# Starting places of the split weights: one fixed place against eight in turn, 32 bytes apart

## The chip, the cores and the metric

The kernel runs on one core of one Trainium2 chip. The metric is the device time of one execution in microseconds (us), taken over several runs. Engines are named as in the profile: PE is the matrix engine (PEld its weight loads), DVE the vector engine, ACT the scalar engine, POOL the general-purpose engine, SP the engine whose queue issues most transfers.

## The reference

One layer of a hybrid decoder: a half-step SwiGLU block, a token mixer of two attentions merged by gates, and a second half-step SwiGLU block, in float32. 256 tokens and 16 meta tokens in front; width 2048, inner width 5632, eight heads of 128 for each attention.

```python
def _swiglu(x, w_gate, w_up, w_down):
    return (jax.nn.silu(x @ w_gate) * (x @ w_up)) @ w_down

def _hybrid_mixer(xn, w_in, b_forget, fox_q_norm, fox_k_norm, w_branch_fox, w_branch_sb, w_out):
    proj = xn @ w_in
    fq, fk, fv, f_logit, sq, sk, sv, g_fox, g_sb = jnp.split(proj, IN_SPLIT_POINTS, axis=-1)
    ...
    merged = jax.nn.sigmoid(g_fox) * (o_fox @ w_branch_fox) + jax.nn.sigmoid(g_sb) * (o_sb @ w_branch_sb)
    return merged @ w_out

    h = h + 0.5 * _swiglu(_rmsnorm(h, ffn1_norm), ffn1_w_gate, ffn1_w_up, ffn1_w_down)
    h = h + _hybrid_mixer(_rmsnorm(h, mix_norm), w_in, b_forget, ...)
    h = h + 0.5 * _swiglu(_rmsnorm(h, ffn2_norm), ffn2_w_gate, ffn2_w_up, ffn2_w_down)
```

## The kernel before

Each float32 product is made of three matmuls. Every operand is split into a high part (rounded to the matrix engine's fp32r type) and a low part (the rest), and `wh x xh`, `wl x xh` and `wh x xl` are summed in PSUM. ACT writes the high part and DVE the low one (`split`, L164 and L165).

All the weights are cut into *units* of 128 rows by 1024 values (two row tiles of 512 columns, as a rule), 753 in all, listed in the order of use (`units`). Three steps run over that list: `load` brings a unit into a `raw` tile (five buffers, SP's queue), `split_unit` makes its parts `wh` and `wl` (three buffers each), and `products` issues its matmuls at L944; `ahead` keeps six loads and two splits ahead of the products. Between matmuls `tick` lets the evacuations, the attention heads and the transposes of other stages go on in small steps. The tile framework orders each engine's instructions and sets the semaphores.

There are three kinds of blocks, and so of matmuls at L944:

- features on PSUM's partitions, 272 tokens: the weight is stationary, 272 columns of an activation part move (FFN1, keys and values);
- the same with 256 tokens (`wide`): `wh` is multiplied with both activation parts in one matmul of 512 columns, `wl` with the high part in one of 256 (queries, `w_out`);
- tokens on the partitions (`by_token`): the activation is stationary, 512 columns of the weight move (gates, branches, FFN2).

Activations lie in slots of one pool, `vals` (25 buffers of 4352 bytes in each partition, tag `v`). A slot holds two tiles, each with a high and a low part behind one another, of 272 columns (the norms of FFN1 and of the mixer) or of 256 (the branches' inputs, FFN2). The gate and query blocks read the mixer's norm, so 272-column parts, though they use 256 tokens. In SBUF the pool of constants comes first, then `vals`, then the weights' pool (`raw`, `wh`, `wl`, 4096 bytes a buffer), then temporaries.

The constants hold an identity and a matrix of ones twice, in float32 (`ident`, `ones`) and in fp32r (`identr`, `onesr`, copied by DVE at L136 and L137), and the first norm's gains apart from the others (`grow1`, `gcol1`). The start is ordered by hand: warm-up matmuls (L293), the transpose of the gains (L297), transposes of x (L312) and of the meta tokens (L303), and the first block's products (L914).

Of the kernel before, what the change touches and what calls it, by code (L numbers as in the profile page):

```python
# [16 lines left out]
P = 128  # L17
# [5 lines left out]
NM = 16  # L23
# [24 lines left out]
def hybrid_layer(ctx: ExitStack, tc: tile.TileContext, x, meta_tokens, ffn1_norm, ffn1_w_gate, ffn1_w_up,  # L48
# [47 lines left out]
            tick()  # L96


    ident = const([P, P], F32, "ident")
    make_identity(nc, ident)  # L100
    ones = const([P, P], F32, "ones")
    nc.gpsimd.memset(ones[:], 1.0)
    eps_c = const([P, 1], F32, "eps")
    nc.gpsimd.memset(eps_c[:], EPS)
    grow = const([64, P], F32, "grow")
    grow1 = const([16, P], F32, "grow1")
    nc.scalar.dma_start(grow1[:], ffn1_norm.rearrange("o (k p) -> (o k) p", p=P))
    for i, g in enumerate((ffn1_norm, mix_norm, ffn2_norm)):
        nc.gpsimd.dma_start(grow[16 * i:16 * i + 16, :], g.rearrange("o (k p) -> (o k) p", p=P))
    nc.gpsimd.dma_start(grow[48:56, :], fox_q_norm[0])  # L110
    nc.gpsimd.dma_start(grow[56:64, :], fox_k_norm[0])
# [4 lines left out]
    def tables():  # L116
        return tc.keep_in_program_order(act.preload_act_table_set(LN_EXP)).ins

    gcol1 = const([P, 16], F32, "gcol1")
    gcol = const([P, 64], F32, "gcol")  # L120
    gq = const([P, 8], F32, "gq")

    identr = const([P, P], F32R, "identr")
    onesr = const([P, P], F32R, "onesr")
    smask = const([P, 2, NR], F32R, "smask")
    urev = const([P, P], F32R, "urev")
    urevm = const([P, P], F32R, "urevm")
# [2 lines left out]
    def other_constants():  # L130
        yield 8
        g_ps = aux()
        pe.transpose(g_ps[:, :64], grow[:], ident[:64, :64])
        dve.tensor_copy(gcol[:], g_ps[:, :64])
        dve.tensor_scalar(gq[:], gcol[:, 48:56], SCALE, None, op0=ALU.mult)
        tc.keep_in_program_order(dve.tensor_copy(identr[:], ident[:]))  # L136
        tc.keep_in_program_order(dve.tensor_copy(onesr[:], ones[:]))  # L137
        tc.keep_in_program_order(dve.tensor_scalar(negone[:], ones[:], -1.0, None, op0=ALU.mult))
        yield 4
        t = temp([P, 2, NT], F32, "F3")  # L140
        nc.gpsimd.memset(t[:], 0.0)
        for i in range(2):
            nc.gpsimd.affine_select(t[:, i, :NR], t[:, i, :NR], pattern=[[1, NR]], compare_op=ALU.is_gt,
                                    fill=NEG, base=-128 * i, channel_multiplier=-1)
        tc.keep_in_program_order(dve.tensor_copy(smask[:], t[:, :, :NR]))
        t = temp([P, 2, NT], F32, "F3")
        nc.gpsimd.memset(t[:, :, :P], 0.0)
        nc.gpsimd.memset(t[:, 0, :P], -1.0)
        nc.gpsimd.affine_select(t[:, 0, :P], t[:, 0, :P], pattern=[[-1, P]], compare_op=ALU.is_ge,
                                fill=0.0, base=0, channel_multiplier=1)  # L150
        for p0 in (0, 32):
            m = t[p0:p0 + 32, 1, :P]
            nc.gpsimd.memset(m, -1.0)
            nc.gpsimd.affine_select(m, m, pattern=[[0, 4], [-1, 32]], compare_op=ALU.is_ge,
                                    fill=0.0, base=0, channel_multiplier=1)
            nc.gpsimd.affine_select(m, m, pattern=[[0, P]], compare_op=ALU.is_ge,
                                    fill=0.0, base=NM - 1, channel_multiplier=-1)
        tc.keep_in_program_order(dve.tensor_copy(urev[:], t[:, 0, :P]))
        tc.keep_in_program_order(dve.tensor_copy(urevm[:], t[:, 1, :P]))
        yield  # L160
# [32 lines left out]
    class Norm:  # L193
# [53 lines left out]
        def by_feature(self):  # L247

            n, ps = self.n, aux()
            pe.matmul(ps[:, :n], ones[:], self.acc[:, :n], start=True, stop=True)  # L250
            y = temp([P, NT], F32, "sq", bufs=2)[:, :n]
            half = temp([P, NT], F32, "half")[:, :n]
            with tc.issue_after(tables()):
                act.activation(y, ps[:, :n], AF.Ln, scale=1.0 / D, bias=eps_c[:])
            act.activation(y, y, AF.Exp, scale=-0.5)
            dve.tensor_scalar(half, ps[:, :n], -0.5 / D, -0.5 * EPS, op0=ALU.mult, op1=ALU.add)
            rsqrt_newton(self.r[:, :n], y, half)
# [16 lines left out]
    warm, msel = first[:, 3, :P], first[:, 3, P:P + NM]  # L274
    msum = const([P, 2], F32, "msum")
    dve.memset(warm, 1.0)

    def load_x(c):
        t = slot([P, 2, 256], F32)
# [14 lines left out]

    def first_gains():
        g_ps = aux()
        pe.transpose(g_ps[:, :16], grow1[:], ident[:16, :16])  # L297
        dve.tensor_copy(gcol1[:], g_ps[:, :16])

    def first_meta():  # L300
        p = aux()
        for h in range(2):
            pe.transpose(p[:, h * P:(h + 1) * P], ms[:, h, :], ident[:])  # L303
        t = p[:, :2 * P].rearrange("p (k t) -> p k t", t=NM)
        dve.tensor_tensor(mgain, t, gcol1[:].unsqueeze(2).to_broadcast([P, KT, NM]), op=ALU.mult)
        return t

    def first_transposes(c):
        ps = [aux(), aux()]
        for i in range(2):  # L310
            for j in range(2):
                pe.transpose(ps[i][:, j * P:(j + 1) * P], xs[c][:, j, i * P:(i + 1) * P], ident[:])  # L312
        return ps

    def first_parts(kt, p):
# [51 lines left out]
            act.activation(s[:], xs[c][:, j, :], AF.Square, accum_out=sums[:, j, c:c + 1])  # L367

    def meta_squares():
        dve.tensor_reduce(msel, ident[:].rearrange("p (k t) -> p t k", t=NM), axis=AX.X, op=ALU.add)  # L370
        for h in range(2):
            s = temp([P, 256], F32, "sq", bufs=2)
            act.activation(s[:, :P], ms[:, h, :], AF.Square, accum_out=msum[:, h:h + 1])

    def first_factors():
        a = temp([P, 4], F32, "st", bufs=4)
        y = temp([P, 4], F32, "st", bufs=4)
        half = temp([P, 4], F32, "st", bufs=4)
        pm = aux()
        for h in range(2):  # L380
            pe.matmul(pm[:NM, :1], msel, msum[:, h:h + 1], start=h == 0, stop=h == 1)
        dve.memset(a[:], 1.0)
        dve.tensor_reduce(a[:, 0:2], sums[:, 0:2, :], axis=AX.X, op=ALU.add)
        dve.tensor_copy(a[:NM, 2:3], pm[:NM, :1])
        act.activation(y[:], a[:], AF.Ln, scale=1.0 / D, bias=eps_c[:])
        act.activation(y[:], y[:], AF.Exp, scale=-0.5)
        dve.tensor_scalar(half[:], a[:], -0.5 / D, -0.5 * EPS, op0=ALU.mult, op1=ALU.add)
        rsqrt_newton(a[:], y[:], half[:])
        diag = temp([P, NT], F32, "half")
        for j in range(2):  # L390
            dve.tensor_scalar(diag[:, j * P:(j + 1) * P], ident[:], a[:, j:j + 1], None, op0=ALU.mult)
        dve.tensor_scalar(diag[:NM, NR:NT], ident[:NM, :NM], a[:NM, 2:3], None, op0=ALU.mult)
        yield 11
        p = aux()
        pe.matmul(p[:, :NR], ones[:], diag[:, :NR], start=True, stop=True)
        pe.matmul(p[:, NR:NT], ones[:NM, :], diag[:NM, NR:NT], start=True, stop=True)
        dve.tensor_copy(norm1.r[:], p[:, :NT])
        norm1.done = True
        yield 2
# [4 lines left out]
    def turn(u, dest, t0):  # L404

        yield 6
        for j0 in range(0, 4, 2):
            p = aux()
            for j in range(2):
                for i in range(2):  # L410
                    c = (j0 + j) * P
                    pe.transpose(p[:, (2 * j + i) * P:(2 * j + i + 1) * P], u[:, i, c:c + P], ident[:])  # L412
            h = slot([P, 2, 2, NR], F32R)
            split(h[:, :, 0, :], h[:, :, 1, :], p[:].rearrange("p (j t) -> p j t", j=2))
            dest[(t0 + j0) // 2] = h
# [141 lines left out]
    def values(v):  # L557
        pv = aux()
        for i in range(3):
            pe.transpose(pv[:, i * P:(i + 1) * P], v[:, i * P:(i + 1) * P], ident[:])  # L560
        vh = temp([P, 384], F32R, "vh", bufs=2)
        vl = temp([P, 384], F32R, "vl", bufs=2)
        split_stacked(vh[:], vl[:], pv[:, :384], 2 * P, 64)
# [80 lines left out]
    def fox_attend(h, t, parts):  # L644
# [23 lines left out]
        for kt in range(3):  # L668
            d = pb if kt == 2 else pa
            for i in range(2):  # L670
                c = (kt % 2) * NR + i * P
                pe.transpose(d[:, c:c + P], pw[:, i, kt * P:(kt + 1) * P], ident[:])  # L672
        split(wh[:, :512], wl[:, :512], pa[:])
        act.activation(wh[:, 512:], pb[:, :NR], AF.Copy)
        stack(wh[:, 512:], pb[:, :NR], 32)
# [146 lines left out]
    def residual_by_token():  # L822
        for c in range(4):
            acc[c] = slot([P, 2, 512], F32)
            for i in range(2):
                ps = aux()
                for j in range(4):
                    pe.transpose(ps[:, j * P:(j + 1) * P], resid(4 * c + j)[:, i * P:(i + 1) * P], ident[:])  # L828
                dve.tensor_copy(acc[c][:, i, :], ps[:])
                yield 4  # L830

# [47 lines left out]
    def load(u):  # L879
# [3 lines left out]
        nc.sync.dma_start(t[:], b.w[rows, b.col0:b.col0 + b.cols].rearrange("(k p) c -> p k c", p=P))  # L883
        raws[u] = t

    def split_unit(u):
        b, k0, n = units[u]
        wh = wp.tile([P, n, b.cols], F32R, tag="wh", name=name("wh"))
        if b.stacked:
            raw, s = raws.pop(u), b.stacked  # L890
            act.activation(wh[:], raw[:], AF.Copy)
            dve.tensor_tensor(wh[:, :, 32:32 + s], raw[:, :, :s], wh[:, :, :s].bitcast(F32), op=ALU.subtract)
            halves[u] = (wh, None)
            return
        wl = wp.tile([P, n, b.cols], F32R, tag="wl", name=name("wl"))
        split(wh[:], wl[:], raws.pop(u)[:])
        halves[u] = (wh, wl)

    def split_half(u, i):
        b, k0, n = units[u]  # L900
        if i == 0:
            halves[u] = tuple(wp.tile([P, n, b.cols], F32R, tag=t, name=name(t)) for t in ("wh", "wl"))
        wh, wl = halves[u]
        split(wh[:, i, :], wl[:, i, :], raws[u][:, i, :])

# [139 lines left out]
```

## Time and profile before

| | |
|---|---|
| median of three runs | 2249.6 us (2248.21 to 2250.57) |
| the profiled execution | 2249.19 us, span 2247.5 us |
| PE busy | 2240.8 us, 13930 matmuls |
| PE weight loads | 2039.6 us |
| DVE / ACT busy | 1265.4 / 1024.6 us |
| DMA | 403.03 MB, mean 179 GB/s |
| TensorE clock granted | 0.999 of full |

A row of a group reads: line, engine, operation, out<-in by the program's names, shape, count | busy us, mean ns of one | idle time of the engine before them. For a matmul the operand named first after the arrow moves and the second is stationary. A row in order of time begins with its start and its length in us; "x2" at its end says that two stand in it. A row of windows has the stretch in us from the span's start, its length, the busy time and count of each engine asked for, the granted clock, the DMA share and GB/s.

### The profile page before, as it was taken

How to read it: one execution, taken by the hardware profiler on the slowest of the kernel's cores; microseconds unless marked ns; L12 is line 12 of the kernel's file. 1: busy time of each engine (PE TensorE's matmuls, PEld its weight loads, DVE VectorE, ACT ScalarE, POOL GpSimd, SP SyncE). 2: the span in 40 equal slices, each digit the busy share in tenths (PEclk: the TensorE clock that was granted, in tenths of full speed). 3: DMA queues.
4: the chain of work that ended last, by engine and by line, in shares of the span. 5: the costliest groups of instructions: out<-in, count | busy, mean ns of one | idle time of the engine just before them, and what ended most of it. 6: DMA issues, size and time to landing. Idle time of an engine off the chain costs nothing.

```text
span 2247.5 us, 34143 instructions
## 1 busy us (share of the span) xinstructions
PE 2240.8 (100%) x13930; PEld 2039.6 (91%) x13930; DVE 1265.4 (56%) x1596; ACT 1024.6 (46%) x1280; POOL 42.1 (2%) x112
## 2 busy tenths in 40 slices
PE   9999999999999999999999999999999999999999
PEld 9999999999999999988899988888888888888887
DVE  6555544455555555987556666675445544544554
ACT  6444433334444454655446564454444433444433
POOL 1000000000000001110000000000000000000000
PEclk9999999999999999999999999999999999999999
DMA  7666655566665566555655556566666666666664
GB/s 228 171 177 178 172 177 177 171 178 176 172 177 175 173 184 180 158 167 167 194 180 151 150 150 187 181 185 178 188 190 193 187 191 194 191 190 190 188 199 156
DMA packets 211325, 403.03 MB, mean 179 GB/s; under 512 B 12680, under 2 KB 17632, under 8 KB 211168
## 3 DMA queue, kind: packets, MB, share of 16 engines
q1 hardware_dynamic: 209088, 397.33, 59.1%
q8 instruction: 109, 1.79, 0.3%
q10 hardware_dynamic: 1472, 2.37, 0.3%
q0 software_dynamic: 608, 1.16, 0.2%
q14 instruction: 48, 0.39, 0.1%
HBM read 398.70 MB, written 2.11 MB: 178 GB/s over the span
## 4 chain that ended last, share of the span: by engine, by line
PE 99%; DMA 0%; SPq 0%; DVE 0%; issue 0%; DVEq 0%; ACT 0%
PE acc L944 96%; PE aux L701 1%; PE aux L572 1%; PE aux L412 1%; PE aux L672 0%; PE aux L560 0%; PE acc L914 0%; DMA v<-in_meta_tokens_dram 0%; PE aux L828 0%; PE aux L312 0%; PE aux L651 0%; PE aux L652 0%; PE aux L653 0%; PE aux L615 0%; PE aux L616 0%; PE aux L238 0%
## 5 line engine op out<-in xcount | busy, mean ns | idle before, releaser
L165 DVE TENSOR_TENSOR wl<-raw,wh 128x1024 fp32r<-128x1024 f32 (+1 forms) x753 | 921.4, 1224 | 857.3 <-ACT wh L164 855.8
L164 ACT ACTIVATE wh<-raw 128x1024 fp32r<-128x1024 f32 (+1 forms) x753 | 797.2, 1059 | 1096.2 <-PE acc L944 1029.7
L944 PE MATMUL acc<-v,wh 128*128 128x272 f32 (+1 forms) x5776 | 1172.9, 298 | 0.0
L944 PEld LDWEIGHTS acc<-v,wh 128*128 128x128 f32 x5776 | 923.6, 189 | 22.7
L944 PE MATMUL acc<-wh,v 128*128 128x512 f32 x2880 | 905.9, 391 | 0.0
L944 PE MATMUL acc<-v,wl 128*128 128x272 f32 (+1 forms) x3128 | 897.0, 287 | 0.0
L944 PEld LDWEIGHTS acc<-wh,v 128*128 128x128 f32 x2880 | 540.6, 188 | 111.7
L944 PEld LDWEIGHTS acc<-v,wl 128*128 128x128 f32 x3128 | 587.4, 188 | 0.4 <-DVE wl L165 0.2
L944 PE MATMUL acc<-wl,v 128*128 128x512 f32 x1440 | 561.3, 390 | 0.0
L944 PEld LDWEIGHTS acc<-wl,v 128*128 128x128 f32 x1440 | 270.5, 188 | 54.6
L164 ACT ACTIVATE v<-aux 128x512 fp32r<-128x512 f32 (+1 forms) x46 | 23.7, 516 | 19.2 <-PE aux L412 11.9
L165 DVE TENSOR_TENSOR v<-aux,v 128x512 fp32r<-128x512 f32 (+1 forms) x46 | 27.4, 595 | 4.3 <-ACT v L164 2.6
L440 DVE TENSOR_TENSOR sq<-acc,rbc 128x272 f32<-128x272 f32 x44 | 19.3, 438 | 18.5 <-PE acc L944 17.3
L431 DVE TENSOR_TENSOR v<-acc,rbc 128x272 f32<-128x272 f32 x44 | 18.0, 436 | 15.7 <-PE acc L944 15.7
L164 ACT ACTIVATE v<-sq 128x272 fp32r<-128x272 f32 x44 | 17.4, 419 | 19.5 <-DVE sq L441 19.5
L432 ACT ACTIVATE v<-v 128x272 f32<-128x272 f32 x44 | 17.5, 424 | 13.8 <-DVE v L431 13.8
L473 DVE SCALAR_TENSOR_TENSOR v<-acc,v 128x272 f32<-128x272 f32 x32 | 12.9, 435 | 12.6 <-PE acc L944 12.6
L441 DVE TENSOR_TENSOR sq<-sq,v 128x272 f32<-128x272 f32 x44 | 19.3, 438 | 0.8
L852 ACT ACTIVATE v<-acc,rtok 128x512 f32<-128x512 f32 x22 | 15.2, 690 | 9.9 <-PE acc L944 9.7
L412 PEld LDWEIGHTS aux<-ident,v 128*128 128x128 f32 x120 | 14.8, 140 | 3.7
L165 DVE TENSOR_TENSOR v<-sq,v 128x272 fp32r<-128x272 f32 x44 | 18.2, 434 | 0.0
L412 PE MATMUL aux<-ident,v 128*128 128x128 f32 x120 | 17.9, 272 | 0.0
(219 smaller groups left out, 725.7 us busy)
## 6 DMA issues: line engine op xcount, KB each, us to landing
raw<-in_ffn_w_up_dram SPq DMA_DIRECT2D x176, 512.0 KB, 3.7
raw<-in_ffn_w_down_dram SPq DMA_DIRECT2D x176, 512.0 KB, 3.9
raw<-in_ffn_w_gate_dram SPq DMA_DIRECT2D x175, 512.0 KB, 3.7
raw<-in_w_in_dram SPq DMA_DIRECT2D x162, 512.0 KB, 3.7
raw<-in_w_out_dram SPq DMA_DIRECT2D x32, 512.0 KB, 3.9
raw<-in_w_branch_fox_dram SPq DMA_DIRECT2D x16, 512.0 KB, 3.9
raw<-in_w_branch_sb_dram SPq DMA_DIRECT2D x16, 512.0 KB, 3.9
v<-in_x_dram SPq DMA_DIRECT2D x8, 256.0 KB, 7.8
```

The lines of the kernel that those rows point to most:

```text
L164: act.activation(hi, src, AF.Copy)
L165: dve.tensor_tensor(lo, src, hi.bitcast(F32), op=ALU.subtract)
L412: pe.transpose(p[:, (2 * j + i) * P:(2 * j + i + 1) * P], u[:, i, c:c + P], ident[:])
L431: dve.tensor_tensor(s, ps[:, :n], norm_of().r[:, :n], op=ALU.mult)
L432: act.activation(s, s, AF.Silu)
L440: dve.tensor_tensor(u, ps[:, :n], norm_of().r[:, :n], op=ALU.mult)
L441: dve.tensor_tensor(u, u, s, op=ALU.mult)
L473: dve.scalar_tensor_tensor(r, ps[:, :NT], 0.5, r, op0=ALU.mult, op1=ALU.add)
L572: pe.matmul(po[:, :NR], a[:, ks], b[:, i * NR:(i + 1) * NR], start=n == 0, stop=n == 6)
L701: pe.matmul(o, a, b, start=start, stop=stop, skip_group_check=True)
L852: act.activation(u["t"][:, i, :], ps[:], AF.Silu, scale=norms["ffn2"].rtok[:, i:i + 1])
L944: pe.matmul(o, a, c, start=first and m == 0, stop=last and m == len(terms) - 1, skip_group_check=wide)
```

## The change

It does four things.

- Each part tile gets 56 columns more, and its 1024 columns begin 0 to 224 bytes behind the tile's start, in steps of 32 bytes: `wh` moves on by a step every 4 units, `wl` every 32, each through eight places in turn. The tiles are so 4320 bytes long.
- Identity and ones are kept once, as fp32r, and read as float32 through `bitcast`. They are made in a temporary (`F3`) and copied by DVE at the start.
- The first norm's gains lie in the first 16 rows of `grow` and columns of `gcol`, and POOL's queue no longer loads them a second time.
- So the constants shrink by 1600 bytes and the part tiles grow by 1344.

```diff
-    ident = const([P, P], F32, "ident")
-    make_identity(nc, ident)
-    ones = const([P, P], F32, "ones")
-    nc.gpsimd.memset(ones[:], 1.0)
+    identr = const([P, P], F32R, "identr")
+    ident = identr[:].bitcast(F32)
+    onesr = const([P, P], F32R, "onesr")
+    ones = onesr[:].bitcast(F32)
+    plain = temp([P, 2, NT], F32, "F3")
+    make_identity(nc, plain[:, 0, :P])
+    nc.gpsimd.memset(plain[:, 1, :P], 1.0)
...
-    grow1 = const([16, P], F32, "grow1")
-    nc.scalar.dma_start(grow1[:], ffn1_norm.rearrange("o (k p) -> (o k) p", p=P))
-    for i, g in enumerate((ffn1_norm, mix_norm, ffn2_norm)):
+    grow1 = grow[:16]
+    nc.scalar.dma_start(grow1, ffn1_norm.rearrange("o (k p) -> (o k) p", p=P))
+    for i, g in enumerate((mix_norm, ffn2_norm), 1):
...
-        tc.keep_in_program_order(dve.tensor_copy(identr[:], ident[:]))
-        tc.keep_in_program_order(dve.tensor_copy(onesr[:], ones[:]))
...
     dve.memset(warm, 1.0)
+    dve.tensor_copy(identr[:], plain[:, 0, :P])
+    dve.tensor_copy(onesr[:], plain[:, 1, :P])
...
+    def part_tile(u, tag):
+
+        b, k0, n = units[u]
+        t = wp.tile([P, n * b.cols + 56], F32R, tag=tag, name=name(tag))
+        o = 8 * (u // {"wh": 4, "wl": 32}[tag] % 8)
+        return t[:, o:o + n * b.cols].rearrange("p (k c) -> p k c", k=n)
+
     def split_unit(u):
         b, k0, n = units[u]
-        wh = wp.tile([P, n, b.cols], F32R, tag="wh", name=name("wh"))
+        wh = part_tile(u, "wh")
...
-        wl = wp.tile([P, n, b.cols], F32R, tag="wl", name=name("wl"))
-        split(wh[:], wl[:], raws.pop(u)[:])
+        wl = part_tile(u, "wl")
+        split(wh, wl, raws.pop(u)[:])
```

The order of the matmuls at L944 and of the splits stays. What moves is at the start. DVE's first instructions before the change (`v` with its number is a slot, `aux` a PSUM bank, `F_1` the temporary `F3`):

```order
L276 MEMSET v_108 128x128
L298 COPY gcol_91<-aux_160 128x16
L305 TENSOR_TENSOR v_108<-aux_171,gcol_91 128x256
L320 SCALAR_TENSOR_TENSOR v_178<-aux_165,gcol_91,v_178 128x256
L165 TENSOR_TENSOR wl_182<-raw_118,wh_181 128x512
```

and after it:

```order
L275 MEMSET v_104 128x128
L277 CAST onesr<-F_1_74 128x128
L276 CAST identr<-F_1_74 128x128
L299 COPY gcol<-aux_158 128x16
L306 TENSOR_TENSOR v_104<-aux_169,gcol 128x256
L321 SCALAR_TENSOR_TENSOR v_176<-aux_163,gcol,v_176 128x256
L164 TENSOR_TENSOR wl_180<-raw_116,wh_179 128x512
```

The two copies, which stood at L136 and L137, now stand ahead of the copy of the first gains, and PE's first transpose waits for them. On POOL, the rows behind the two constants were

```order
masks.py:199 AFFINE_SELECT ident<-ident 128x128
L104 MEMSET eps 128x1
L109 DMA grow<-in_ffn_norm_dram 16x128
L109 DMA grow<-in_mix_norm_dram 16x128
L109 DMA grow<-in_ffn_norm_dram 16x128
```

and are

```order
masks.py:199 AFFINE_SELECT F_1_74<-F_1_74 128x128
L107 MEMSET eps 128x1
L112 DMA grow<-in_mix_norm_dram 16x128
L112 DMA grow<-in_ffn_norm_dram 16x128
L113 DMA grow<-in_fox_q_norm_dram 8x128
```

so one transfer fewer stands ahead of the others.

More of the change, by code (lines that the diff above doesn't have):

```diff
@@ L117, in tables @@
         return tc.keep_in_program_order(act.preload_act_table_set(LN_EXP)).ins
-    gcol1 = const([P, 16], F32, "gcol1")
     gcol = const([P, 64], F32, "gcol")
+    gcol1 = gcol[:, :16]
     gq = const([P, 8], F32, "gq")
-    identr = const([P, P], F32R, "identr")
-    onesr = const([P, P], F32R, "onesr")
     smask = const([P, 2, NR], F32R, "smask")
@@ L133, in other_constants @@
         pe.transpose(g_ps[:, :64], grow[:], ident[:64, :64])
-        dve.tensor_copy(gcol[:], g_ps[:, :64])
+        dve.tensor_copy(gcol[:, 16:], g_ps[:, 16:64])
         dve.tensor_scalar(gq[:], gcol[:, 48:56], SCALE, None, op0=ALU.mult)
-        tc.keep_in_program_order(dve.tensor_copy(identr[:], ident[:]))
-        tc.keep_in_program_order(dve.tensor_copy(onesr[:], ones[:]))
-        tc.keep_in_program_order(dve.tensor_scalar(negone[:], ones[:], -1.0, None, op0=ALU.mult))
+        tc.keep_in_program_order(dve.tensor_scalar(negone[:], ones, -1.0, None, op0=ALU.mult))
         yield 4
@@ L249, in by_feature @@
             n, ps = self.n, aux()
-            pe.matmul(ps[:, :n], ones[:], self.acc[:, :n], start=True, stop=True)
+            pe.matmul(ps[:, :n], ones, self.acc[:, :n], start=True, stop=True)
             y = temp([P, NT], F32, "sq", bufs=2)[:, :n]
@@ L296, in first_gains @@
         g_ps = aux()
-        pe.transpose(g_ps[:, :16], grow1[:], ident[:16, :16])
-        dve.tensor_copy(gcol1[:], g_ps[:, :16])
+        pe.transpose(g_ps[:, :16], grow1, ident[:16, :16])
+        dve.tensor_copy(gcol1, g_ps[:, :16])
     def first_meta():
@@ L302, in first_meta @@
         for h in range(2):
-            pe.transpose(p[:, h * P:(h + 1) * P], ms[:, h, :], ident[:])
+            pe.transpose(p[:, h * P:(h + 1) * P], ms[:, h, :], ident)
         t = p[:, :2 * P].rearrange("p (k t) -> p k t", t=NM)
-        dve.tensor_tensor(mgain, t, gcol1[:].unsqueeze(2).to_broadcast([P, KT, NM]), op=ALU.mult)
+        dve.tensor_tensor(mgain, t, gcol1.unsqueeze(2).to_broadcast([P, KT, NM]), op=ALU.mult)
         return t
@@ L311, in first_transposes @@
             for j in range(2):
-                pe.transpose(ps[i][:, j * P:(j + 1) * P], xs[c][:, j, i * P:(i + 1) * P], ident[:])
+                pe.transpose(ps[i][:, j * P:(j + 1) * P], xs[c][:, j, i * P:(i + 1) * P], ident)
         return ps
@@ L369, in meta_squares @@
     def meta_squares():
-        dve.tensor_reduce(msel, ident[:].rearrange("p (k t) -> p t k", t=NM), axis=AX.X, op=ALU.add)
+        dve.tensor_reduce(msel, ident.rearrange("p (k t) -> p t k", t=NM), axis=AX.X, op=ALU.add)
         for h in range(2):
@@ L390, in first_factors @@
         for j in range(2):
-            dve.tensor_scalar(diag[:, j * P:(j + 1) * P], ident[:], a[:, j:j + 1], None, op0=ALU.mult)
+            dve.tensor_scalar(diag[:, j * P:(j + 1) * P], ident, a[:, j:j + 1], None, op0=ALU.mult)
         dve.tensor_scalar(diag[:NM, NR:NT], ident[:NM, :NM], a[:NM, 2:3], None, op0=ALU.mult)
@@ L394, in first_factors @@
         p = aux()
-        pe.matmul(p[:, :NR], ones[:], diag[:, :NR], start=True, stop=True)
+        pe.matmul(p[:, :NR], ones, diag[:, :NR], start=True, stop=True)
         pe.matmul(p[:, NR:NT], ones[:NM, :], diag[:NM, NR:NT], start=True, stop=True)
@@ L411, in turn @@
                     c = (j0 + j) * P
-                    pe.transpose(p[:, (2 * j + i) * P:(2 * j + i + 1) * P], u[:, i, c:c + P], ident[:])
+                    pe.transpose(p[:, (2 * j + i) * P:(2 * j + i + 1) * P], u[:, i, c:c + P], ident)
             h = slot([P, 2, 2, NR], F32R)
@@ L559, in values @@
         for i in range(3):
-            pe.transpose(pv[:, i * P:(i + 1) * P], v[:, i * P:(i + 1) * P], ident[:])
+            pe.transpose(pv[:, i * P:(i + 1) * P], v[:, i * P:(i + 1) * P], ident)
         vh = temp([P, 384], F32R, "vh", bufs=2)
@@ L671, in fox_attend @@
                 c = (kt % 2) * NR + i * P
-                pe.transpose(d[:, c:c + P], pw[:, i, kt * P:(kt + 1) * P], ident[:])
+                pe.transpose(d[:, c:c + P], pw[:, i, kt * P:(kt + 1) * P], ident)
         split(wh[:, :512], wl[:, :512], pa[:])
@@ L827, in residual_by_token @@
                 for j in range(4):
-                    pe.transpose(ps[:, j * P:(j + 1) * P], resid(4 * c + j)[:, i * P:(i + 1) * P], ident[:])
+                    pe.transpose(ps[:, j * P:(j + 1) * P], resid(4 * c + j)[:, i * P:(i + 1) * P], ident)
                 dve.tensor_copy(acc[c][:, i, :], ps[:])
@@ L884, in load @@
         raws[u] = t
+    def part_tile(u, tag):
[3 more added lines that the diff above has]
+        return t[:, o:o + n * b.cols].rearrange("p (k c) -> p k c", k=n)
     def split_unit(u):
         b, k0, n = units[u]
-        wh = wp.tile([P, n, b.cols], F32R, tag="wh", name=name("wh"))
+        wh = part_tile(u, "wh")
         if b.stacked:
             raw, s = raws.pop(u), b.stacked
-            act.activation(wh[:], raw[:], AF.Copy)
+            act.activation(wh, raw[:], AF.Copy)
             dve.tensor_tensor(wh[:, :, 32:32 + s], raw[:, :, :s], wh[:, :, :s].bitcast(F32), op=ALU.subtract)
@@ L901, in split_half @@
         if i == 0:
-            halves[u] = tuple(wp.tile([P, n, b.cols], F32R, tag=t, name=name(t)) for t in ("wh", "wl"))
+            halves[u] = tuple(part_tile(u, t) for t in ("wh", "wl"))
         wh, wl = halves[u]
```

## Prediction

> **What bounds the kernel now.** I read the page's busy times, the chain that ended last and the waits of PE first, then the groups of matmuls by shape, then single matmuls in order of time, because the first views leave only one question: how far apart two matmuls start.
>
> ```profile
> span 2247.5 us, 34143 instructions
> PE 2240.8 (100%) x13930; PEld 2039.6 (91%) x13930; DVE 1265.4 (56%) x1596; ACT 1024.6 (46%) x1280; POOL 42.1 (2%) x112
> PEclk9999999999999999999999999999999999999999
> PE 99%; DMA 0%; SPq 0%; DVE 0%; issue 0%; DVEq 0%; ACT 0%
> ```
>
> ```profile
> PE aux L303 <- DMA v<-in_meta_tokens_dram: 1.4, 2, 0.8
> PE aux L293 <- DVE v L276: 1.1, 1, 1.1
> PE acc L914 <- ACT v L326: 0.3, 1, 0.3
> ```
>
> PE is 99% of the chain, its clock is full, and in the whole span it waits for others 2.8 us. The profiled execution took 2249.19 us, 0.4 below the median of 2249.6; sums are made against the former and the result is given against the median. "Busy 100%" says that a matmul is always under way, not that it streams all the time: the price of a matmul is the distance to the next start. Its columns cannot change here, so only that distance can.
>
> ```profile
> L944 PE MATMUL acc<-v,wh 128*128 128x272 f32 x5264 | 991.4, 288 | 0.0
> L944 PE MATMUL acc<-wh,v 128*128 128x512 f32 x2880 | 905.9, 391 | 0.0
> L944 PE MATMUL acc<-v,wl 128*128 128x272 f32 x2616 | 753.4, 289 | 0.0
> L944 PE MATMUL acc<-wl,v 128*128 128x512 f32 x1440 | 561.3, 390 | 0.0
> L944 PE MATMUL acc<-v,wh 128*128 128x512 f32 x512 | 181.8, 398 | 0.0
> L944 PE MATMUL acc<-v,wl 128*128 128x256 f32 x512 | 143.7, 281 | 0.0
> ```
>
> Three kinds, then. The name behind the arrow is the moving operand, the second the stationary one. 7880 matmuls (x5264 and x2616) move 272 activation columns over a weight tile; 4320 (x2880 and x1440) move 512 columns of a weight tile over an activation tile (the by-token blocks); 1024 are the pairs of 512 and 256. Windows whose ends I set at starts of matmuls give the pace of each kind; the count in the row takes in the two to four that hang over an end.
>
> ```profile
> 48.98:809.95 760.97, 760.97 (x6062) 1.00 0.59 175
> 1340.99:1387.71 46.72, 46.72 (x206) 1.00 0.64 192
> 1787.09:1959.94 172.85, 172.85 (x766) 1.00 0.63 192
> ```
>
> The first is FFN1: 760.97 us by 6060 is 125.6 ns for 272 columns. The third is FFN2: 172.85 by 762 is 226.8 ns for 512 columns. Between the two lie 240 columns and 101.2 ns, 0.42 ns a column; 272 columns are so worth some 115 ns, and about 11 ns of every matmul are start-up. That is all the change can touch: 13930 of them are some 150 us if they all went, and they have no reason to go.
>
> **What depends on the place.** I call "place" the byte at which an operand begins, modulo 256, counted from where the activation slots begin. It is worked out from the sizes in the code. A slot is 4352 bytes (17 x 256) and a weight tile 4096, and the pools lie one behind the other, so before the change every slot and every weight tile begins at place 0. A 272-column part is 1088 bytes (4 x 256 + 64), so the four parts in a 272-wide slot begin at 0, 64, 128 and 192; in a 256-wide slot all at 0. So the code already holds stretches that differ in nothing but the places. The first two rows are FFN2 (everything at 0); the next two are from the gate blocks, which move the same weights over 272-wide activation slots (stationary at 0, 64, 128, 192).
>
> ```profile
> 1810.56 0.39 PE L944 MATMUL acc<-wl,v 128*128 128x512 f32 x1
> ...
> 1811.92 0.39 PE L944 MATMUL acc<-wl,v 128*128 128x512 f32 x1
> ...
> 1361.23 0.39 PE L944 MATMUL acc<-wl,v 128*128 128x512 f32 x1
> ...
> 1363.99 0.39 PE L944 MATMUL acc<-wl,v 128*128 128x512 f32 x1
> ```
>
> A wl matmul comes every third. FFN2: six matmuls in 1.36 us, 226.7 ns each. Gates: twelve in 2.76 us, 230.0 ns; over the whole stretch 1340.99 to 1387.71 (204 inside) 229.0. Same columns, same clock, same engines beside it: mixed places cost 2.3 to 3.3 ns a matmul.
>
> Against this stand two others. In the next fence the first two rows are w_out (pairs of 512 and 256, all at place 0), the last two the query blocks (the same pairs, moving parts at 0 and 64 or 128 and 192).
>
> ```profile
> 1433.26 0.28 PE L944 MATMUL acc<-v,wl 128*128 128x256 f32 x1
> ...
> 1434.32 0.28 PE L944 MATMUL acc<-v,wl 128*128 128x256 f32 x1
> ...
> 1118.87 0.28 PE L944 MATMUL acc<-v,wl 128*128 128x256 f32 x1
> ...
> 1120.27 0.28 PE L944 MATMUL acc<-v,wl 128*128 128x256 f32 x1
> ```
>
> Three pairs in 1.06 us are 353.3 ns a pair with one place; four in 1.40 us are 350.0 with several: here mixing is cheaper by 1.7 ns a matmul, though the query blocks' 512 columns are two pieces of 256. And inside FFN1:
>
> ```profile
> 299.82 0.29 PE L944 MATMUL acc<-v,wl 128*128 128x272 f32 x1
> ...
> 300.20 0.29 PE L944 MATMUL acc<-v,wl 128*128 128x272 f32 x1
> ...
> 300.57 0.29 PE L944 MATMUL acc<-v,wl 128*128 128x272 f32 x1
> ...
> 300.95 0.29 PE L944 MATMUL acc<-v,wl 128*128 128x272 f32 x1
> ```
>
> Threes take 0.38 and 0.37 us in turn, as the slots' halves (parts at 0 and 64; at 128 and 192) take turns. So the place counts, by a few ns, and the sign is open.
>
> Here the Trainium skill would have it otherwise. "TensorE: Matmul & The Clock Gate", Part 2, step 1, says that PE has two independent read ports, and that "Loading the next tile's weights doesn't steal SBUF read bandwidth from the running matmul". By that no two places could meet, the change would be worth nothing, and the sum would be 2249.6. The rows above show that equal matmuls differ by 3 ns with the place; whether the two ports meet, or each begins dearer at some places, they do not show.
>
> **The change part by part.** *The places.* A part tile grows to 4320 bytes (32 short of 17 x 256), so the three buffers of a tag begin 32 bytes apart, and an offset of 0 to 224 bytes is added, which moves on every 4 units for wh and every 32 for wl. The two run through their combinations almost evenly. Terms:
>
> (a) 512 columns, everything at place 0 now: 4320 less the 768 of the gates (2 kinds x 4 blocks x 16 x 2 x 3), so 3552. Afterwards wh and wl are at any of eight places against a fixed activation. Not in the trace; ends: -2.7 ns (the 0.38 against the 0.37 us of three in FFN1, if one place were all dear and the others all cheap) and +3.3 (gates, 230.0 against 226.7). I take the middle of the gates' two values, 229.5 less 226.7, +2.8, since these are the same matmuls in the same orientation: 3552 x 2.8 = +9.9 us.
>
> (b) 272 columns, 7880: they see four places already, evenly. Eight instead of four gives the same mean if a step of 32 is like a step of 64; no row shows odd multiples. Ends: all like the faster threes (0.37 us against a mean of 0.375, -1.7 ns, -13 us) and +19 us (rival 2). I take 0.
>
> (c) The pairs: w_out's 512 matmuls (256 pairs) go from 353.3 to 350.0, -0.8 us; the query blocks stay. (d) The gates' 768 are mixed already: 0.
>
> *Identity and ones.* Two casts on DVE move from 49.9 us to the start, POOL issues one DMA less, and the first transposes now wait for DVE.
>
> ```profile
> 1.19 0.29 POOL masks.py:199 TENSOR_SCALAR_AFFINE_SELECT ident<-ident 128x128 f32<-128x128 f32 x1
> 1.57 0.65 POOL L109 DMA_DIRECT2D grow<-in_ffn_norm_dram  x1
> 3.98 0.13 PEld L297 LDWEIGHTS aux<-ident,grow 16*128 16x128 f32 x1 [0.22 <-issue]
> 6.75 0.14 PEld L303 LDWEIGHTS aux<-ident,v 128*128 128x128 f32 x1 [0.78 <-DMA v<-in_meta_tokens_dram]
> L136 DVE CAST identr<-ident x1: 223/223/223, 49.9 to 49.9; 128x128 fp32r<-128x128 f32 x1
> ```
>
> POOL is done at 1.48; two casts of 0.22 end by 2.0, and the first transposes start at 3.98, held by the gains' DMA: cover 2 us. Behind the casts on DVE stands nothing before the copy of the gains (after 3.98). The first products wait for the meta tokens (6.75) anyway. Cost 0; if the cover went, at most 0.45 us. The DMA not issued moves POOL's later issues up by 0.65 us, and the rest of the gains is not read before some 49 us: 0. At 49.9 us DVE loses 0.45 us of work under busy PE: 0.
>
> *ACT and DVE write at 32-byte steps.* No row shows such a write. The cover is the chain's 99% of PE, and where DVE is fullest it still has 12% free:
>
> ```profile
> 900.00:1000.00 100.00, 88.22 (x166) 1.00 0.54 156
> ```
>
> A dearer write would have to cost an eighth there before anything waits; I take 0, with no lower end since PE does not wait for it now.
>
> Sum: 9.9 - 0.8 = +9.1 us: 2258.3 in a profiled execution, 2258.7 against the median.
>
> **The rivals.** *1, faster:* place 0 against place 0 is the dear pair, as w_out against the query blocks and the two halves in FFN1 have it, and the gates are dear for their changing stationary operand. Then (a) is -1.7 ns x 3552 = -6.0, (c) -0.8: 2242.8; with -2.7 ns, 2239.2. It decides if FFN2's pace falls under 226.7. Against it: the gates.
>
> *2, slower and in FFN1:* what costs in the gates is that the stationary operand's place changes from one matmul to the next (four changes in six, so 2.8 x 6/4 = 4.2 ns a change). FFN1 has none now, as wh and wl both begin at 0; afterwards two of every three steps go between wh and wl, and 7 of 8 combinations differ: 7880 x 2/3 x 7/8 x 4.2 = +19.3, FFN2 unchanged, with (c) 2268.1. For it: the gates alone have such changes. Against: the gates' equal steps are no faster than the unequal ones as far as rows at 10 ns show.
>
> *3, nothing:* the mean over eight places is the present mean, or (a) and (b) cancel: 2249.6, within 4.5 us. For it: FFN1, the longest stage, is mixed already.
>
> **How the numbers follow.** The forecast (mixed places cost in FFN2 as in the gates) 0.34; rival 2 0.18; rival 1 0.28; nothing 0.20. 0.2% of 2249.6 is 4.5 us, about what three runs tell from no change. Faster 0.28, same 0.20, slower 0.52. The range goes from rival 1's end, 2239, to 2273: it holds rival 2's 2268 and leaves out its sum with (a), 2278. The forecast's own range is 2253 (1.2 ns, the gates' lower value less 1) to 2261 (3.3 ns).
>
> **What the next profile would show.** FFN2's window at 229 to 230 ns a matmul if (a) holds, 224 to 225 if rival 1; and paces that step with the unit's place, every 4 units. FFN1's window at 125.6 if (b) holds, about 128 if rival 2. The chain still 99% PE, and the first products near 7.9 us. What would make the forecast wrong above all is the odd multiples of 32, which nothing in this trace shows, and that a mean over combinations need not lie where four places put it.

## The result, and the profile after

The changed kernel takes 2265.05 us (median of three runs, 2263.95 to 2265.21) against 2249.6 before: ratio 1.0068, 95% interval 1.0052 to 1.0084. It is 15.4 us slower.

The page's lines on the span, the engines and the chain that ended last:

```profile
span 2263.3 us, 34142 instructions
PE 2258.0 (100%) x13930; PEld 2039.2 (90%) x13930; DVE 1265.1 (56%) x1596; ACT 1024.3 (45%) x1280; POOL 40.8 (2%) x111
PE 99%; DMA 0%; ACT 0%; SPq 0%; issue 0%; DVE 0%; DVEq 0%
```

The span grew by 15.8 us, PE's busy time by 17.2; weight loads, DVE and ACT are as before. The matmuls by shape (L952 is the line that was L944):

```profile
L952 PE MATMUL acc<-v,wh 128*128 128x272 f32 x5264 | 990.2, 288 | 0.1
L952 PE MATMUL acc<-wh,v 128*128 128x512 f32 x2880 | 917.7, 395 | 0.0
L952 PE MATMUL acc<-v,wl 128*128 128x272 f32 x2616 | 751.5, 288 | 0.0
L952 PE MATMUL acc<-wl,v 128*128 128x512 f32 x1440 | 566.8, 394 | 0.0
```

Only the groups in which 512 weight columns move (`wh,v` and `wl,v`) are longer, by 4 ns each; the 272-column groups are 1.2 and 1.9 us shorter. The pace, the distance from one matmul's start to the next, says it better. The rows are two stretches of four units in FFN2 (units 592 to 595 and 596 to 599, counted from 0; 48 matmuls each), then the windows of FFN1 (6060 inside), `w_out` (484) and FFN2 (762) between the same matmuls as before:

```profile
1804.40:1815.48 11.09, 11.09 (x49) 1.00 0.64 188
1815.48:1826.61 11.12, 11.12 (x49) 1.00 0.62 189
49.26:808.99 759.73, 759.73 (x6062) 1.00 0.59 175
1426.52:1511.09 84.57, 84.57 (x488) 1.00 0.62 190
1793.18:1969.91 176.73, 176.73 (x765) 1.00 0.63 188
```

FFN1: 125.4 ns (125.6 before). `w_out`: 174.7 a matmul, 349.5 a pair. FFN2: 176.73 by 762 is 231.9 ns where it was 226.8. It hardly steps from one stretch of four units to the next: 231.0 and 231.7 ns in the two shown, 230.2 to 232.7 in the 40 that no transpose disturbs. Single units run from 227.2 to 234.3: the three buffers of a tag begin 32 bytes apart, so `wh` and `wl` change their places from unit to unit, not only every 4 and 32. The clock is 1.00 in every row.

All distances between matmul starts, added up by kind from the two traces, account for the 15.8 us of the span. A distance counts for a kind when both its matmuls are products of that kind's blocks; the last row has all the others:

| kind | before, us | after, us | difference |
|---|---|---|---|
| branches and FFN2, 512 columns (3515 distances) | 801.0 | 817.8 | +16.8 |
| gates, 512 columns | 169.4 | 170.4 | +1.0 |
| 272 columns (7845 distances) | 986.6 | 985.6 | -1.0 |
| `w_out`, pairs | 90.4 | 89.3 | -1.0 |
| queries, pairs | 88.6 | 88.9 | +0.3 |
| everything else on PE | 106.2 | 105.9 | -0.3 |

At the start, PE's and DVE's rows in order of time:

```profile
3.98 0.28 PE L298 MATMUL aux<-identr,grow 16*128 16x16 f32 x1
...
7.85 0.59 PE L922 MATMUL acc<-v,wh 128*128 128x272 f32 x1
```

```profile
1.19 0.23 DVE L277 CAST onesr<-F 128x128 fp32r<-128x128 f32 x1
1.60 0.23 DVE L276 CAST identr<-F 128x128 fp32r<-128x128 f32 x1 [0.18 <-POOL eps L107]
```

The two casts are done at 1.83 us, 2.15 before the first transpose, which starts at 3.98 as before.

The splits, which now write at 32-byte steps, take as long as they did. Before and after:

```profile
L165 DVE TENSOR_TENSOR wl<-raw,wh 128x1024 fp32r<-128x1024 f32 x751 | 920.0, 1225 | 857.3 <-ACT wh L164 855.8
L164 ACT ACTIVATE wh<-raw 128x1024 fp32r<-128x1024 f32 x751 | 796.0, 1060 | 1096.2 <-PE acc L944 1029.7 <-issue 57.5 <-ACT sq L220 2.6
...
L164 DVE TENSOR_TENSOR wl<-raw,wh 128x1024 fp32r<-128x1024 f32 x751 | 919.5, 1225 | 872.8 <-ACT wh L163 871.4
L163 ACT ACTIVATE wh<-raw 128x1024 fp32r<-128x1024 f32 x751 | 795.7, 1060 | 1110.5 <-PE acc L952 1042.7 <-issue 56.1 <-ACT sq L219 3.6
```

### The profile page after: what moved, and what is told of

Read it like the earlier page. It is cut to its first block, busy times and chain, and to the rows that moved or that the text cites. A ratio compares the mean times of both kernels' runs of the same rounds, so it can differ in the third digit from the quotient of the medians.

```text
span 2263.3 us, 34142 instructions
## 1 busy us (share of the span) xinstructions
PE 2258.0 (100%) x13930; PEld 2039.2 (90%) x13930; DVE 1265.1 (56%) x1596; ACT 1024.3 (45%) x1280; POOL 40.8 (2%) x111
## 4 chain that ended last, share of the span: by engine, by line
PE 99%; DMA 0%; ACT 0%; SPq 0%; issue 0%; DVE 0%; DVEq 0%
PE acc L952 96%; PE aux L702 1%; PE aux L573 1%; PE aux L413 1%; PE aux L673 0%; PE aux L561 0%; DMA v<-in_meta_tokens_dram 0%; PE aux L829 0%; PE acc L922 0%; PE aux L313 0%; PE aux L616 0%; PE aux L654 0%; PE aux L652 0%; PE aux L653 0%; PE aux L617 0%; ACT wh L163 0%
## 5 line engine op out<-in xcount | busy, mean ns | idle before, releaser
L952 PE MATMUL acc<-v,wh 128*128 128x272 f32 (+1 forms) x5776 | 1171.0, 298 | 0.1
L952 PEld LDWEIGHTS acc<-v,wh 128*128 128x128 f32 x5776 | 919.5, 188 | 22.5 <-ACT wh L163 0.5
L952 PE MATMUL acc<-wh,v 128*128 128x512 f32 x2880 | 917.7, 395 | 0.0
L952 PE MATMUL acc<-v,wl 128*128 128x272 f32 (+1 forms) x3128 | 895.0, 287 | 0.0
L952 PEld LDWEIGHTS acc<-wh,v 128*128 128x128 f32 x2880 | 540.8, 188 | 123.6
L952 PEld LDWEIGHTS acc<-v,wl 128*128 128x128 f32 x3128 | 587.9, 188 | 0.4 <-DVE wl L164 0.2
L952 PE MATMUL acc<-wl,v 128*128 128x512 f32 x1440 | 566.8, 394 | 0.0
L952 PEld LDWEIGHTS acc<-wl,v 128*128 128x128 f32 x1440 | 270.6, 188 | 60.0
L413 PEld LDWEIGHTS aux<-identr,v 128*128 128x128 f32 x120 | 14.9, 140 | 3.9
L413 PE MATMUL aux<-identr,v 128*128 128x128 f32 x120 | 18.0, 272 | 0.0
```

Of the source, the lines that this page charges most:

```text
L952: pe.matmul(o, a, c, start=first and m == 0, stop=last and m == len(terms) - 1, skip_group_check=wide)
```

## The experiments

All kernels are the changed kernel with other places. In most of them the part tile is padded by 64 columns, to 4352 bytes, so that every buffer begins at place 0 and `o` (in float32 elements, 4 bytes each) is the whole of the place. The theory (P in the expectations) was that the pace follows from the weight's place against the activation's, and that for 512 moving weight columns equal places are best. Against it stood: the layout or identity and ones (L); the change of place between `wh` and `wl` from one matmul to the next (C, and in FFN1 S, rival 2 of the prediction); and the weight's own address, whatever the activation's (A). The medians of the kernel before beside these runs were 2248.97, 2249.14 and 2249.38 us, and 2250.01 (one run) beside the ninth.

**1. Everything of the change, all places 0.**

```diff
-        t = wp.tile([P, n * b.cols + 56], F32R, tag=tag, name=name(tag))
-        o = 8 * (u // {"wh": 4, "wl": 32}[tag] % 8)
+        t = wp.tile([P, n * b.cols + 64], F32R, tag=tag, name=name(tag))
+        o = 0
```

> The changed kernel with its parts all at place 0 (offset 0, part tiles of 4352 bytes), identity and ones kept once as in the change. Theory P (what costs is the place of a weight part counted from that of the activation): the whole loss goes, 2249.6 within 3 us, FFN2 at 226.8 ns a matmul. Rival L (the new layout costs: the single identity, the slots' new absolute address): the time stays at 2262 to 2265.

2249.21 us (10 runs), ratio 1.0001 (0.9992 to 1.0011). FFN1 and FFN2:

```profile
48.25:809.20 760.95, 760.95 (x6061) 1.00 0.58 175
1786.67:1959.50 172.83, 172.83 (x766) 1.00 0.62 192
```

125.6 and 226.8 ns, as before. Identity, ones, gains, moved pools and larger tiles cost nothing together that stands out of the interval (-1.8 to +2.5 us), and FFN2's pace is back to the tenth of a nanosecond; the 15.4 us are the places'. L falls.

**2. `wh` and `wl` walk together.** Same tile, and

```diff
+        o = 8 * (u // 4 % 8)
```

> wh and wl walk through the eight places together, a step every 4 units, so that two successive matmuls never see weights at different places. Theory P: FFN2 takes 226.8 ns at place 0 and 233 to 236 at the seven others, as where the two coincided in the changed kernel (228.3, then 232.8 to 236.4); its mean is 233 and the time 2249.6 + 3552 x 6.2 ns = 2271 or so. Rival C (what costs is that wh and wl lie at different places, so that the place changes from matmul to matmul): no loss, 2250, every place at 227.

2269.48 us (one run), 20.5 above the kernel before: with no change between `wh` and `wl` the loss is larger, not gone. C falls. Since both stand at one place for four units, the map can be read from windows, here 24 matmuls each in FFN2, at places 0, 32, 64 and so on to 224:

```profile
2035.73:2041.17 5.44, 5.44 (x25) 1.00 0.65 184
2046.69:2052.29 5.60, 5.60 (x25) 1.00 0.67 195
2057.85:2063.34 5.49, 5.49 (x25) 1.00 0.65 186
2069.80:2075.40 5.60, 5.60 (x25) 1.00 0.62 186
2080.99:2086.57 5.57, 5.57 (x25) 1.00 0.64 186
2092.17:2097.79 5.62, 5.62 (x25) 1.00 0.61 187
2103.41:2109.01 5.60, 5.60 (x25) 1.00 0.64 186
2115.48:2121.08 5.60, 5.60 (x25) 1.00 0.63 185
```

By 24: 226.7, 233.3, 228.8, 233.3, 232.1, 234.2, 233.3 and 233.3 ns. Place 0 is alone; the odd multiples of 32 are all at 233 or above. The mean of the eight is 231.9, what FFN2 has in the changed kernel. The rows below are `w_out` at 224, 0 and 32 (30, 30 and 32 matmuls):

```profile
1478.14:1483.35 5.20, 5.20 (x32) 1.00 0.59 191
1489.28:1494.58 5.30, 5.30 (x32) 1.00 0.60 193
1500.59:1506.24 5.65, 5.65 (x34) 1.00 0.74 217
```

Place 0 is among the dearest there, at 176.7 ns a matmul, but not alone: 32 takes the same, and so does 64 in its undisturbed pairs. The cheapest are 96 and 224, at 173.3. At 272 columns the places lie between 124.8 (192) and 126.7 (64).

**3. Both parts fixed at 128.** As 1, with `o = 32`.

> All weight parts at one fixed place, 128, halfway between two activation places of 256. Theory P: FFN2 and the branches at about 234 ns, 3552 x 7.2 = +26 us, the other stages as before: 2275. Rival C, or a rival in which the moving from place to place costs: 2250, since nothing moves.

2267.89 us (4 runs), ratio 1.0082 (1.0067 to 1.0097). FFN1, FFN2:

```profile
48.20:809.15 760.95, 760.95 (x6061) 1.00 0.58 175
1794.58:1971.74 177.16, 177.16 (x766) 1.00 0.62 188
```

FFN2 takes 232.5 ns with nothing that walks or changes, so the rival in which the change costs falls. Theory P has the direction, but its 234 ns and 2275 us were too much, by 7 us in the time. FFN1 takes 125.6, as at 0.

**4. The change's walk for all but the by-token blocks.**

```diff
+        o = 0 if b.by_token else 8 * (u // {"wh": 4, "wl": 32}[tag] % 8)
```

> The eight places walk as in the change in the blocks whose weight is stationary (FFN1, keys, values, queries, w_out); in the by-token blocks (gates, branches, FFN2) all parts lie at place 0. Theory P: the loss goes and the small gain of the other blocks stays, 2249.6 - 0.8 (pairs) - 1.0 (272 columns) = 2247.8. Rival S (the stationary operand's change of place costs, in FFN1): most of the loss stays, 2260 to 2265.

2248.33 us (10 runs), ratio 0.9997 (0.9987 to 1.0006).

```profile
49.35:809.48 760.13, 760.13 (x6061) 1.00 0.58 175
1786.39:1959.22 172.83, 172.83 (x765) 1.00 0.63 192
```

With FFN1's weights walking through all combinations its pace is 125.4 ns, and FFN2's is back at 226.8. The whole loss lies in the by-token blocks, and rival 2 (S) falls.

**5. Steps of 4 bytes.** As 2, with `o = u // 4 % 8`, so places 0 to 28.

> wh and wl walk together through eight places 4 bytes apart (0 to 28), a step every 4 units. If the place counts in steps of 32 bytes, all eight are as good as place 0: 2249, FFN2 at 226.8 throughout. If every byte offset breaks the good relation, FFN2 takes 226.8 at 0 alone and some 233 at the seven others, 2269 as when the steps were 32 bytes. If it counts in 16 bytes, half of it: 0 to 12 at 226.8 and 16 to 28 dearer, 2260.

2270.15 us (one run), 21.0 above. FFN2 at places 0, 4, 20 and 28, 24 matmuls each:

```profile
2127.02:2132.46 5.44, 5.44 (x25) 1.00 0.68 192
2138.03:2143.73 5.70, 5.70 (x25) 1.00 0.66 191
...
2183.61:2189.37 5.76, 5.76 (x25) 1.00 0.83 292
...
2206.22:2211.68 5.47, 5.47 (x25) 1.00 0.60 180
```

226.7, 237.5, 240.0 and 227.9 ns. One element is enough, and a place 4 bytes off is dearer than one 32 bytes off. The time is that of the second case, but the seven places are not alike: 28 bytes off cost 1.2 ns, 20 bytes off 13.3, twice what was expected.

**6. Everything at 0, and all slots and weights shifted alike.** As before, a tile of 4096 bytes, and 128 bytes more of constants:

```diff
+    fill = const([P, 32], F32, "fill")
+    dve.memset(fill[:], 0.0)
```

> A constant of 128 bytes is put ahead of the slots, so that slots and weight parts all begin at multiples of 256 bytes of the partition; against the run with weights alone moved by 128 the weights stand at the same address and the slots do not. Theory P (only the relation between weight and activation counts): 2249, FFN2 at 226.8. Rival A (the weight's address itself counts, and its multiple of 256 is the dear one): 2268, as when the weights alone were moved by 128.

2249.22 us (10 runs), ratio 1.0003 (0.9994 to 1.0012).

```profile
47.84:808.80 760.96, 760.96 (x6061) 1.00 0.59 175
1786.52:1959.38 172.86, 172.86 (x765) 1.00 0.64 192
```

By the programs' addresses modulo 256, slots and weights begin at 192 in the kernel before, at 128 in experiment 1 (1600 bytes of constants less) and at 0 here (128 bytes more): FFN2's pace is 226.8 ns in all three. Moving both operands by 64 or 128 bytes together changes nothing, while moving the weights alone by 128 costs 5.7 ns (experiment 3). So it isn't the weight's own address.

**7. Another place for each kind.** The places are chosen from the map of experiment 2:

```diff
+    def place(b):
+        if b.by_token:
+            return 4 if b.w is wi and b.kts == KT else 0
+        if b.n == NT:
+            return 6
+        return 4 if b.w is wi else 7
...
+        o = 8 * place(b)
```

So 192 for 272 columns, 128 for gates and queries, 224 for `w_out`, 0 for branches and FFN2.

> Each kind of block has a fixed place, wh and wl alike, the cheapest seen in the run in which they walked together: 192 for the 272-column blocks (124.85 ns against 125.33 at 0 inside a unit), 0 for branches and FFN2, 128 for the gates, 224 for w_out's pairs, 128 for the query pairs. Theory P: 7880 x -0.48 = -3.8 us, w_out -1.6, queries -0.4, gates -0.9; together -6.7 us, 2242.3. If a kind settles into another of its rhythms than in that run, the gain is less, down to none: 2249.

2242.81 us (9 runs), ratio 0.9974 (0.9964 to 0.9983): 6.3 us below the kernel before, the shortest median of all versions. FFN1, `w_out`, FFN2:

```profile
48.45:804.92 756.47, 756.47 (x6061) 1.00 0.60 176
1420.25:1504.22 83.97, 83.97 (x487) 1.00 0.62 191
1780.85:1953.68 172.83, 172.83 (x765) 1.00 0.63 192
```

124.8, 173.5 and 226.8 ns. From the traces, the 272-column distances fell from 986.6 to 982.2 us and the distances of `w_out`'s pairs from 90.4 to 88.7; that is 6.1 of the 6.3. Place 128 did not bring what the expectation gave it: the gates' distances rose from 169.4 to 170.1 us where 0.9 less was expected, and those of the query pairs stayed (88.6 and 88.7). So the expected -6.7 came out partly by luck: the 272 columns gave 4.4 us instead of 3.8, and PE's distances outside the product blocks, which were not counted on, 0.9.

**8. The activation moves instead.** Weights at 0; FFN2's and `w_out`'s activation parts lie 272 columns apart, so at 0, 64, 128 and 192.

```diff
-            h = slot([P, 2, 2, NR], F32R)
-            split(h[:, :, 0, :], h[:, :, 1, :], p[:].rearrange("p (j t) -> p j t", j=2))
+            h = slot([P, 2, 2, NT], F32R)
+            split(h[:, :, 0, :NR], h[:, :, 1, :NR], p[:].rearrange("p (j t) -> p j t", j=2))
```

> The weights stay at place 0; the activation parts of FFN2 and of w_out are laid into the slots 272 columns apart, as those of the gates are, so that they begin at 0, 64, 128 and 192 in turn. Theory P: FFN2's 3168 matmuls take the gates' 229 to 230 ns, +7 to +10 us, and w_out's pairs 350.0 as the queries' do, -0.8 us: 2256 to 2259. Rival A (the weight's address alone counts): 2249.

2258.70 us (4 runs), ratio 1.0040 (1.0027 to 1.0054).

```profile
48.28:809.23 760.95, 760.95 (x6061) 1.00 0.59 175
1789.19:1964.53 175.34, 175.34 (x765) 1.00 0.63 190
```

FFN2 takes 230.1 ns with weights that stand where they stood before the change. The mean of experiment 2's places 0, 64, 128 and 192 is 230.2. A falls, and with experiment 6 what is left for the by-token blocks is the place of one operand against the other.

**9. Every 4 bytes up to 256.** As 2, with `o = u // 4 % 65`.

> wh and wl walk together through 65 places 4 bytes apart, 0 to 256, a step every 4 units: the whole map of places for the 272-column and the by-token blocks in one look. If the relation repeats after 256 bytes, place 256 is as cheap as place 0 (226.7 ns in FFN2); if it repeats later, 256 is one more dear place (233). The mean over the places is taken as in the two walks before: 2268 to 2272. Open: whether any place is cheaper than 0 for FFN2, or than 124.8 ns for 272 columns.

2271.55 us (one run), 21.5 above. The rows are FFN1 at places 56, 64, 184 and 192 (72 matmuls each), then by-token blocks at 256, 20 and 128 (24 each):

```profile
185.63:194.67 9.04, 9.04 (x74) 1.00 0.62 176
209.72:218.84 9.12, 9.12 (x74) 1.00 0.60 172
570.17:579.13 8.96, 8.96 (x74) 1.00 0.63 180
595.53:604.65 9.12, 9.12 (x74) 1.00 0.61 172
1594.64:1600.08 5.44, 5.44 (x25) 1.00 0.68 200
1662.98:1668.74 5.76, 5.76 (x25) 1.00 0.62 183
1967.04:1972.64 5.60, 5.60 (x25) 1.00 0.65 188
```

256 is as good as 0 (226.7 ns), 128 isn't (233.3), so the pattern repeats after 256 bytes at the earliest. Of the 65 places none other than 0 and 256 is below the 227.8 of 28, 60 and 108; 20, 116, 196 and 244 take 240.0. With 272 columns the cheapest seemed to be 116, 184 and 244, 124.4 ns.

This map also tests the theory at 272 columns. There the activation parts begin at 0, 64, 128 and 192; `wh` meets all four, `wl` the two high parts, at 0 and 128. So weights at a place and at the place 128 bytes further meet the same differences modulo 256, and by the theory they should take the same time. Of the 31 such pairs of places with an undisturbed stretch of 72 matmuls, 27 agree within 0.2 ns (64 and 192 both take 126.7). The four that do not are 12 and 140, 40 and 168, 56 and 184, 80 and 208. Two readings stand out: 184 has 124.4 where its partner 56 has 125.6, and 192 has 126.7 here where experiments 2 and 7 have 124.8. The place is so not all that sets the pace: the same place can run at two.

**10 and 11. The map's cheapest places for 272 columns.** Fixed places, 184 bytes in one and 244 in the other, with `w_out` at 224 and the rest at 0:

```diff
+        if b.n == NT:
+            return 46      # 61 in the other
+        return 0 if b.w is wi else 56
```

> Places by kind, from the map of 65: 184 for the 272-column blocks (124.44 ns inside a unit against 125.56 at 0), 224 for w_out's pairs (346.7 ns against 353.3), 0 for all the rest. Theory P with the map's numbers: 7880 x -1.1 = -8.7 us, 256 pairs x -6.6 = -1.7: 2239. If the map's rhythm is not the one into which whole blocks settle, somewhere between that and the run with 192 (2242.8).

> The same with 244 for the 272-column blocks, the other place at which the map has 124.44 ns: 2239 if the map's number holds, 2243 if not.

Both missed. With 184: 2246.72 us (11 runs), ratio 0.9988 (0.9979 to 0.9997). With 244: 2251.21 (11 runs), ratio 1.0005 (0.9996 to 1.0015). FFN1 of the first:

```profile
48.76:809.72 760.96, 760.96 (x6061) 1.00 0.54 175
```

and of the second:

```profile
49.95:814.28 764.34, 764.34 (x6061) 1.00 0.54 174
```

125.6 and 126.1 ns, where stretches of 72 at the same places took 124.4 in experiment 9. What 184 gains is mostly `w_out`'s (1.7 of 2.7 us). A pace read from a short stretch, entered from another place, isn't always the one in which a whole block settles: the block at 184 took the 125.6 of its partner 56, and at 192 it settled at the 124.8 of experiment 2, not at the 126.7 of experiment 9. At 128 all took 125.6. One of the eleven runs at 244 took 2240.41 us, with the others between 2249.96 and 2253.03; it left no trace, so whether FFN1 ran at 124.4 ns there stays open.

## Why the prediction was right, and where its size was off

The direction, the mechanism and the place in the program held: 2258.7 was forecast, within 2239 to 2273, and 2265.05 came out. It lies above the forecast's own range of 2253 to 2261, and nearer to rival 2's 2268 than to the forecast; the wide range holds it because rival 2 stretched it upwards, not because the main term did. The time alone would not tell the two apart; the windows do, since the loss lies in FFN2 and FFN1 is no slower. By its steps:

- *Only the distance between matmul starts can change.* Held. The chain is 99% PE as before, and the distances account for the whole difference (table above).
- *Term (a), the 512 weight columns in branches and FFN2.* The sign and the comparison were right, the size was not: +2.8 ns were taken, +4.8 measured (227.87 to 232.66 over 3515 distances), +16.8 us instead of +9.9. This is the mis-sized term. The gates, from which it was taken, show places 0, 64, 128 and 192 only. Experiment 8 puts FFN2 at just these and gets 230.1, +3.3, the upper end of the gates' values. The change adds the odd multiples of 32, at 233.3 to 234.2 in experiment 2, and the mean of all eight is 231.9. It was the risk that the prediction named; its upper end for this term, +3.3, was too low, because it took the stretch with some good places as the bound for places that it had no row of. Its lower end, -2.7, does not follow from its rows either: 0.38 against 0.37 us of three are 3.3 ns a matmul, and rows rounded to 10 ns carry no more than that.
- *Term (b), 272 columns: 0.* Held, to -1.0 us. The places differ (124.8 to 126.7), but the walk's mean (125.4 ns in FFN1) is close to what place 0 gives against the activation's four (125.6).
- *Term (c), `w_out`: -0.8.* Held: -1.0. *Term (d), gates: 0.* Measured +1.0.
- *Identity and ones, POOL's DMA, writes at 32-byte steps: 0.* Held, by experiment 1 for the first two. The writes took 1225 and 1060 ns on DVE and ACT before and after, and in experiment 4, where they walk outside the by-token blocks, nothing is lost. The cover at the start was 2.15 us.
- *Rival 1* (place 0 against 0 is the dear pair) is half true where the activation moves in 512 columns (`w_out`: 176.7 ns at 0, among the dearest, as at 32) and false where the weight moves (FFN2: 226.7, the cheapest). The prediction's two contradicting rows were both right, and the by-token blocks have far more matmuls. Whether the orientation decides is not separated: `w_out`'s matmuls also differ in their columns (pairs of 512 and 256).
- *Rival 2* (a change of place between `wh` and `wl`) fell: FFN1 keeps 125.4 ns with the walk (experiment 4), and FFN2 loses without any change (experiment 3).
- *Rival 3* fell as a whole, but it is right for 7880 of the matmuls, to 1.0 us.
- *Paces that step every 4 units* did not show: the three buffers bring several places into every four units (230.2 to 232.7).

By the Trainium skill's statement in "TensorE: Matmul & The Clock Gate", Part 2, step 1, that a weight load takes no read bandwidth from the running matmul, taken as the prediction took it, the time would have stayed at 2249.6. Measured, the pace of equal matmuls runs from 226.7 to 240.0 ns with the place of one operand against the other. Whether the next weight load and the moving stream hinder each other, or something else depends on the difference of their addresses, no run here separates: each matmul here has its own weight load (13930 of each).

## What to carry to other kernels

Where matmuls run back to back with a weight load each, the distance between starts, read from a window of hundreds of them, is the number to watch: PE's busy share (100%) and its waits show nothing of the 5.1 ns that each of FFN2's matmuls lost. The alignment modulo 256 bytes of the moving operand against the stationary one is worth trying by kind of matmul (here 0.26% of the time, for a pad and a constant), and a walk through many places gave FFN2 the mean of the places (231.9 ns), not the best. A price taken from places that the trace happens to hold bounds only these, and a place found in a short stretch has to be timed over a whole block.

## What the runs showed of the hardware that was not expected

- The pace depends on single elements: 226.7 ns at 0, 237.5 at 4 bytes, 240.0 at 20, 227.9 at 28, and 226.7 again at 256.
- The sign depends on the kind of matmul: equal places are the cheapest for 512 moving weight columns (226.7 ns) and among the dearest for `w_out`'s pairs (176.7 ns a matmul, against 173.3).
- At 272 columns places 128 bytes apart, which meet the same differences, share their pace in 27 of 31 pairs.
- The distances repeat in short fixed rhythms, to the nanosecond of the trace: 227, 227, 226 at place 0 in FFN2. At 128 in experiment 2 there are two: 238, 229, 238, 229, 237, 229 in the stretch near 1992 us (mean 233.3) and twelve between 228 and 241 near 2083 us (mean 232.1). What selects the rhythm is open; it may be behind the misses of experiments 10 and 11, and behind the two paces at 192.
